# The last store of a batched q·kᵀ kernel, issued as a DMA of three quarters of every row and two for the rest, of 125 and 3 partitions

## The chip, the cores and the metric

One core of a Trainium2 chip. The metric is the device time of one execution, in microseconds (us); lower is better.

## The reference

```python
q, k: (8, 12, 1024, 64) float32
def reference(q, k):
    return np.einsum('bhid,bhjd->bhij', q, k).astype(np.float32)
```

That is 96 heads, each a 1024 x 1024 product over 64. The output is 402.65 MB, the input 50.33 MB: a kernel that mostly writes.

## The kernel before

Inputs are loaded and cast to float16, transposed on VectorE, multiplied on TensorE, copied from PSUM by ScalarE into an output tile of 32 KB per partition, and each finished head goes out as one 4 MB store on the SyncE queue. Three output tiles rotate. What matters here:

```python
out_pool = ctx.enter_context(tc.tile_pool(name="out_pool", bufs=3))
...
def scores(self, n, side):
    ...
    o_sb = out_pool.tile([P, NT, S], F32, tag="out")     # 128 x 8 x 1024
    for u in range(NT // 2):
        ...                                              # 4 matmuls into ps
        pin(nc.scalar.copy(out=dst, in_=ps))             # all but the first heads
        ...
    pin(
        nc.sync.dma_start(
            out=of[self.first + n].rearrange("(p t) j -> p (t j)", p=P),
            in_=o_sb.rearrange("p t j -> p (t j)"),
        )
    )
```

Row 8p + t of a head lies in partition p, so each partition's row of 8192 elements is contiguous in memory on both sides.

## Time and profile before

| | before |
|---|---|
| time | 1066.99 us, median of 3 runs (1066.63 to 1067.32) |
| span of the profiled core | 1065.3 us |
| DMA | 425 GB/s mean over the span, 430 GB/s in the steady part |
| busiest compute engines | PE 66%, ScalarE 65% |
| last store issued, first and last of its 16 landings, end of span | 1042.44, 1053.39, 1063.95, 1065.30 us |

A DMA of this kernel is spread over up to 16 DMA engines. In the traces an engine's packets follow one another, and after the last comes a 4-byte completion write, whose landing raises the semaphore of the DMA by one. The trace keeps the time of every such landing, so the landings of one DMA show when each of its engines finished, but not which engine it was. In the views, a DMA share of 1.00 means all 16 engines are busy, 0.06 is one engine.

### The profile page before, as it was taken

How to read it: one execution, taken by the hardware profiler on the slowest of the kernel's cores; microseconds unless marked ns; L12 is line 12 of the kernel's file. 1: busy time of each engine (PE TensorE's matmuls, PEld its weight loads, DVE VectorE, ACT ScalarE, POOL GpSimd, SP SyncE). 2: the span in 40 equal slices, each digit the busy share in tenths (PEclk: the TensorE clock that was granted, in tenths of full speed). 3: DMA queues.
4: the chain of work that ended last, by engine and by line, in shares of the span. 5: the costliest groups of instructions: out<-in, count | busy, mean ns of one | idle time of the engine just before them, and what ended most of it. 6: DMA issues, size and time to landing. Idle time of an engine off the chain costs nothing.

```text
span 1065.3 us, 4306 instructions
## 1 busy us (share of the span) xinstructions
PE 700.8 (66%) x1568; PEld 240.8 (23%) x1568; DVE 427.0 (40%) x57; ACT 694.5 (65%) x384; POOL 354.5 (33%) x206
## 2 busy tenths in 40 slices
PE   5886757667576665766667566675766757778770
PEld 2222222222222222222222222222222222222220
DVE  3767750480191084058029108405702910940000
ACT  2776667576675766757666675666757667777771
POOL 7666350523505225052250532505325053200000
DMA  9999999999999999999999999999999999999996
GB/s 381 433 430 432 429 433 432 432 429 432 431 426 435 430 428 431 431 430 430 431 429 431 432 429 428 432 431 429 430 431 429 430 429 433 431 432 428 431 433 273
DMA packets 27382, 453.28 MB, mean 425 GB/s; under 512 B 3040, under 2 KB 3040, under 8 KB 14304
## 3 DMA queue, kind: packets, MB, share of 16 engines
q1 hardware_dynamic: 15120, 407.90, 89.0%
q10 hardware_dynamic: 12240, 45.09, 10.4%
q8 instruction: 12, 0.20, 0.1%
q14 instruction: 10, 0.08, 0.0%
HBM read 50.33 MB, written 402.65 MB: 425 GB/s over the span
## 4 chain that ended last, share of the span: by engine, by line
DMA 71%; ACT 17%; PE 7%; POOL 1%; DVE 1%; issue 1%; ACTq 0%; POOLq 0%
DMA out_dram<-o_sb 70%; ACT o_sb L169 17%; PE ps L158 7%; POOL half_sb L114 1%; DMA early<-in_k_dram 1%; DVE kT L131 0%; DVE o_sb L165 0%; DVE o_sb L167 0%; ACT o_sb L164 0%; ACT L164 0%; ACTq L169 0%; DVE kT L142 0%; PE ps L139 0%; ACTq L77 0%; POOLq L114 0%
## 5 line engine op out<-in xcount | busy, mean ns | idle before, releaser
L158 PE MATMUL ps<-kT,qT 64*128 64x512 f16 x1536 | 696.9, 617 | 333.1 <-ACT o_sb L169 326.2
L169 ACT COPY o_sb<-ps 128x2048 f32<-128x2048 f32 x379 | 689.2, 1869 | 333.3 <-DMA out_dram<-o_sb 303.9
L114 POOL CAST half_sb<-x_sb 32x2048 f16<-32x2048 f32 x176 | 332.5, 1889 | 549.9 <-DMA x_sb<-in_k_dram 517.5
L158 PEld LDWEIGHTS <-qT 64*128 64x128 f16 x1536 | 237.4, 157 | 790.7 <-issue 788.4
L131 DVE STREAM_TRANSPOSE qT<-half_sb 128x2048 f16<-128x2048 f16 (+1 forms) x24 | 213.2, 8884 | 496.6 <-POOL half_sb L114 496.6
L131 DVE STREAM_TRANSPOSE kT<-half_sb 128x2048 f16<-128x2048 f16 (+1 forms) x24 | 215.7, 8988 | 0.0
L114 POOL CAST half_sb<-early 32x1024 f16<-32x1024 f32 x16 | 16.6, 1036 | 2.2 <-DMA early<-in_k_dram 1.5
L164 ACT ACT_TABLE_LOAD x1 | 1.3, 1283 | 11.7 <-DMA early<-in_k_dram 11.7
L139 PE MATMUL ps<-ident,half_sb 128*128 128x128 f16 x32 | 3.9, 309 | 6.6 <-POOL half_sb L96 6.1
L165 DVE COPY o_sb<-ps 128x1024 f32<-128x1024 f32 x4 | 4.8, 1222 | 6.9 <-ACT o_sb L164 6.9
L96 POOL CAST half_sb<-early 128x512 f16<-128x512 f32 x8 | 4.7, 616 | 3.8 <-DMA early<-in_q_dram 3.8
L164 ACT COPY o_sb<-ps 128x1024 f32<-128x1024 f32 x4 | 4.0, 1014 | 3.0 <-PE ps L158 3.0
L142 DVE COPY qT<-ps 128x1024 f16<-128x1024 f16 x2 | 2.4, 1220 | 7.1 <-PE ps L139 7.1
L139 PEld LDWEIGHTS <-half_sb 128*128 128x128 f16 x32 | 3.3, 142 | 8.1 <-POOL half_sb L96 6.1
L142 DVE COPY kT<-ps 128x1024 f16<-128x1024 f16 x2 | 2.4, 1220 | 3.8 <-PE ps L139 3.8
L167 DVE COPY o_sb<-ps 128x2048 f32<-128x2048 f32 x1 | 2.3, 2291 | 2.0 <-PE ps L158 2.0
masks.py:199 POOL TENSOR_SCALAR_AFFINE_SELECT ident<-ident 128x128 f16<-128x128 f16 x1 | 0.3, 294 | 0.1
masks.py:197 POOL MEMSET ident<- 128x128 f16 x1 | 0.2, 205 | 0.3 <-POOLq L277 0.3
L277 POOL MEMSET const-float32-0.0<- 128x1 f32 x1 | 0.1, 98 | 0.2 <-issue 0.2
L277 POOL MEMSET const-bfloat16-1.0<- 128x1 bf16 x1 | 0.1, 102 | 0.0
L277 POOL MEMSET const-uint8-127<- 128x1 uint8 x1 | 0.1, 102 | 0.0
L277 POOL MEMSET const-float32-1.0<- 128x1 f32 x1 | 0.1, 98 | 0.0
## 6 DMA issues: line engine op xcount, KB each, us to landing
out_dram<-o_sb SPq DMA_DIRECT2D x96, 4096.0 KB, 25.6
x_sb<-in_q_dram ACTq DMA_DIRECT2D x38, 512.0 KB, 24.7
x_sb<-in_k_dram ACTq DMA_DIRECT2D x38, 512.0 KB, 24.7
x_sb<-in_q_dram SPq DMA_DIRECT2D x3, 1024.0 KB, 14.7
x_sb<-in_k_dram ACTq DMA_DIRECT2D x3, 1024.0 KB, 15.2
early<-in_q_dram SPq DMA_DIRECT2D x4, 256.0 KB, 4.9
early<-in_k_dram ACTq DMA_DIRECT2D x4, 256.0 KB, 5.0
early<-in_q_dram SPq DMA_DIRECT2D x2, 512.0 KB, 7.6
```

Source lines behind the costliest of these rows:

```text
L96: nc.gpsimd.tensor_copy(out=self.halves[x][:, :, half], in_=self.raw[half][:, x].rearrange("p (r d) -> p r d", d=D),)
L114: nc.gpsimd.tensor_copy(out=dst[:, :, b % 2], in_=raw[32 * b : 32 * b + 32, :, :, h],)
L131: pin(nc.vector.transpose(out=dst, in_=src))
L139: pin(nc.tensor.transpose(t_ps[:, t], self.halves[x][:, t], ident))
L142: pin(nc.vector.tensor_copy(out=dst, in_=src))
L158: nc.tensor.matmul(ps[:, tt, js], qT[cs, g, 2 * u + tt], kT[cs, g, js])
L164: pin(nc.scalar.copy(out=dst[:, 0], in_=ps[:, 0]))
L165: pin(nc.vector.tensor_copy(out=dst[:, 1], in_=ps[:, 1]))
L167: pin(nc.vector.tensor_copy(out=dst, in_=ps))
L169: pin(nc.scalar.copy(out=dst, in_=ps))
L277: nc = _bacc.Bacc("TRN2", target_bir_lowering=False, num_devices=1)
```

## The change

Its intent can be read from its shape: at the end of the program the engines stop one after another, and a quarter of the last store is taken from all 16 and given to a few.

```diff
-            pin(
-                nc.sync.dma_start(
-                    out=of[self.first + n].rearrange("(p t) j -> p (t j)", p=P),
-                    in_=o_sb.rearrange("p t j -> p (t j)"),
-                )
-            )
+            dst = of[self.first + n].rearrange("(p t) j -> p t j", p=P)
+            parts = [(slice(P), slice(NT))]
+            if self.first + n == BH - 1:
+                rest = slice(NT - 2, NT)
+                parts = [
+                    (slice(P), slice(NT - 2)),
+                    (slice(125), rest),
+                    (slice(125, P), rest),
+                ]
+            for ps, ts in parts:
+                pin(nc.sync.dma_start(out=dst[ps, ts], in_=o_sb[ps, ts]))
```

The other 95 stores, and every instruction of the compute engines, stay as they are.

## The prediction

> **What bounds the kernel now.** I read the page first, part 2 (the span in 40 slices), then the DMA queues and issues, then the chain of waits, and last the end of the span in narrow windows.
>
> ```profile
> DMA  9999999999999999999999999999999999999996
> GB/s 381 433 430 432 429 433 432 432 429 432 431 426 435 430 428 431 431 430 430 431 429 431 432 429 428 432 431 429 430 431 429 430 429 433 431 432 428 431 433 273
> DMA packets 27382, 453.28 MB, mean 425 GB/s; under 512 B 3040, under 2 KB 3040, under 8 KB 14304
> ...
> DMA 71%; ACT 17%; PE 7%; POOL 1%; DVE 1%; issue 1%; ACTq 0%; POOLq 0%
> ...
> out_dram<-o_sb SPq DMA_DIRECT2D x96, 4096.0 KB, 25.6
> ```
>
> The 16 DMA engines are over 90% busy in 39 of 40 slices at about 430 GB/s, while no compute engine is above 66%. The bytes are fixed: 402.65 MB of output and 50.33 MB of input. So the only time that is not already filled with transfers is at the two ends, and the fortieth slice (6 tenths, 273 GB/s) is the end the change works on. Cut into windows of the trace (columns: stretch in us, its length, busy time and count of PE, PEld, DVE, ACT, POOL, clock, DMA share, GB/s), that slice looks so:
>
> ```profile
> 1052.00:1053.00 1.00, 0.00 (x0) 0.00 (x0) 0.00 (x0) 0.00 (x0) 0.00 (x0) 1.00 0.91 393
> 1053.00:1054.00 1.00, 0.00 (x0) 0.00 (x0) 0.00 (x0) 0.00 (x0) 0.00 (x0) 1.00 0.69 295
> 1054.00:1056.00 2.00, 0.00 (x0) 0.00 (x0) 0.00 (x0) 0.00 (x0) 0.00 (x0) 1.00 0.49 213
> 1056.00:1058.00 2.00, 0.00 (x0) 0.00 (x0) 0.00 (x0) 0.00 (x0) 0.00 (x0) 1.00 0.27 115
> 1058.00:1060.00 2.00, 0.00 (x0) 0.00 (x0) 0.00 (x0) 0.00 (x0) 0.00 (x0) 1.00 0.15 66
> 1060.00:1062.00 2.00, 0.00 (x0) 0.00 (x0) 0.00 (x0) 0.00 (x0) 0.00 (x0) 1.00 0.04 16
> 1062.00:1064.00 2.00, 0.00 (x0) 0.00 (x0) 0.00 (x0) 0.00 (x0) 0.00 (x0) 1.00 0.04 16
> ```
>
> Nothing computes any more, and the DMA share falls in steps for ten microseconds. It is not one transfer slowing down; it is 16 engines stopping one after another. The trace's record of semaphore landings says the same more sharply. The last store lands 16 times, once per engine, at 1053.39, 1053.42, 1053.46, 1053.86, 1053.95, 1054.96, 1055.19, 1055.26, 1055.83, 1056.12, 1057.38, 1058.06, 1058.44, 1059.93, 1060.54 and 1063.95 us. The store before it shows nearly the same spread, 1043.64 to 1054.30, so the order of the engines is a lag built up over the whole kernel, and each engine takes about 9.7 us for its 256 KiB. One engine is 3.41 us behind the second slowest, and alone it sets the end. The last instruction of the queue and the wait that ends the program:
>
> ```profile
> 1042.44 0.33 SPq L173 DMA_DIRECT2D out_dram<-o_sb  x1
> ...
> SPq L288 <- DMA out_dram<-o_sb: 21.1, 3, 9.6
> ```
>
> The store is issued at 1042.44, before even the fastest engine has finished the one before it (1043.64), so no engine runs dry. After the last landing 1.35 us remain to the end of the span at 1065.30 (closing barrier).
>
> **What the Trainium skill says.** First, "DMA: Bandwidth & Descriptors", section "Why a DMA increments its semaphore by 16 and not by 1": a DMA uses the largest k up to 16 that divides the slowest dimension of both sides, on the lowest-numbered k engines; 127 partitions give 1. The trace agrees for 128 partitions: 96+38+38+3+3+4+4+2+2 = 190 DMAs times 16 completion writes are the 3040 packets under 512 B. By that rule 125 partitions go to 5 engines (0 to 4) and 3 to 3 engines (0 to 2); no DMA of the kernel before tests it. Second, the same page, "Latency and other measured facts": engines 7 and 15 are usually slower than the others, with a cause that the page calls a guess and ties to another kind of queue. The trace shows one clear laggard but not its number. Third, "SBUF — State Buffer", "Door 1: The DMA port swizzle": eight partitions share one DMA port of about 27.2 GB/s, and a 128-partition transfer gives each engine a port of its own. The packet records agree with the rate: 32,768 B in 1.213 us (median) is 27.0 GB/s. They can't say whether the engine or the port sets it, and that matters below.
>
> **The change part by part.** The order of instructions shows 95 stores untouched, and the ninety-sixth replaced by three DMAs on the same queue: 128x6144, 125x2048 and 3x2048 elements. PE, ACT, DVE and POOL keep their instructions. Everything up to 1042.4 us should be as before.
>
> Removed: each engine's eight 32 KB packets become eight of 24 KB. At 1.213 us per 32 KB that is 0.909 us each, 8 x 0.304 = 2.43 us less on each of the 16 engines.
>
> Added, on engines 0 to 4: 25 packets of 8 KB. The trace has 384 packets of 8 KB on this queue (loads), median 0.313 us, so 7.83 us. Engines 0 to 2 get one more, 0.31 us. Net per engine: 5 to 15 -2.43 us; 3 and 4 +5.40; 0 to 2 +5.71.
>
> Added, on the issuing side: two more issues of 0.33 us at 1042.8 and 1043.1. Their data is needed only when an engine has done its 24 KB packets, over 7 us later: hidden. Their two semaphores were last used eight DMAs earlier, so no wait. The closing waits name these semaphores already; I allow 0.1 us.
>
> Sum, if engines 0 to 4 are the five early ones (there are exactly five within 0.56 us, then a gap of 1.0): laggard 1063.95 - 2.43 = 1061.52; second slowest 1058.11; the five at most 1053.95 + 5.71 = 1059.66. The laggard still ends last, with 1.9 us to spare. The end moves by -2.43 us plus 0.1: 1064.66 us, -0.22%. The most that perfect balance could give is the laggard's distance to the mean of the 16 landings (1056.46), 7.5 us or 0.7%. So a gain over 2% (21 us) is impossible through this part of the time.
>
> **The rivals.**
> *The wrong engines.* Nothing in this profile numbers the engines. An engine that gets +5.71 stays under 1061.52 only if it landed before 1055.81, which eight of sixteen do. If one of the five is today's 1057.38, the end is 1063.1 (gain 0.9); at 1058.44 it is 1064.2 (+0.2); at 1060.54 it is 1066.3 (+2.3, time 1069.3); if the laggard itself is one, +5.7 and a time of 1072.7. For it: five drawn blindly would mostly include a late one. Against it: a split as odd as 125 and 3 looks chosen to reach the five engines known to be early, and the skill's usual slow ones are 7 and 15.
>
> *The ports.* The five engines now read partitions outside their own port. If the rate is the port's and not the engine's, bytes per port are unchanged: the laggard's port has 256 KiB left at 1054.30 as before, whoever reads them, and while the laggard is busy every visitor slows it. Then the gain vanishes: about 0, time 1067.0, and if the five are held up by busy ports, up to 1 to 3 us slower. For it: 27.0 measured is within 1% of the page's port figure. Against it: an engine may have the same limit, and both then look alike; no transfer of the kernel before crosses ports.
>
> *One engine only.* If the rule gave k = 1 for 125 partitions, 125 x 0.313 = 39.1 us would sit on one engine: 1053.4 - 2.4 + 39.1 = 1090.1 for an early one, +26 us, a time near 1093, slower by 2.4%. 125 = 5 x 25, so the rule speaks against it; I leave 2%.
>
> *Hidden anyway?* No: nothing but this store runs after 1042.4, so what the laggard gains is gained.
>
> **Range and chances.** I give the full gain (about 1064.6) 45%; a part of it, through one misplaced engine or partial port sharing (1065 to 1066.8), 15%; no gain by ports (about 1067) 20%; a loss of 1 to 6 us 18%; one engine only 2%. The median lies just above the full gain: 1065.2. Eight in ten: 1064.0 to 1069.5; the low end is the full gain with 0.6 us for spread between runs (0.7 us in the three runs before), the high end takes in all but the worst placements. Faster by over 2% is excluded by the 7.5 us bound; 0.5% stays for what I don't see. Slower by over 2% needs the one-engine case: 2%.
>
> **What would show it.** In the changed kernel's profile: packets 27382 - 144 + 280 = 27518 (280 = 128 + 125 + 3 data and 16 + 5 + 3 completion writes), and 3048 under 512 B instead of 3040, if k is 5 and 3; 3042 would mean k = 1 twice. The 6144-element store should take 16 landings ending near 1061.5, some 2.4 us sooner, and the 125-partition one five landings between 1058.8 and 1059.7. Placement wrong: the five landings come after 1061.5 and set the end. Ports: the five land late and spread out, the 16 gain less than 2.4 us, and 8 KB packets on the queue take clearly more than 0.313 us, up to twice that. The windows after 1060 should have more than one engine's share (0.06) if the load is better spread.

## The result, and the profile after

The changed kernel takes 1073.09 us (median of 4 runs, 1072.15 to 1073.29), against 1067.0 us (4 runs) of the kernel before. The ratio is 1.0055, 95% interval 1.0038 to 1.0073, so it is slower by half a per cent. Here and below a ratio is the mean time of one kernel's fast runs over the mean of the other's of the same rounds, so it is not quite the ratio of the medians. The forecast of 1065.2 us and its range of 1064.0 to 1069.5 both missed.

The page of the changed kernel, parts 2 (the slices), 4 (the chain that ended last, by engine) and 6 (the DMA issues):

```profile
DMA  9999999999999999999999999999999999999994
GB/s 381 441 427 431 430 429 436 425 432 430 432 435 425 434 426 435 433 428 432 429 430 427 429 439 422 434 433 425 433 427 433 427 434 434 430 432 432 429 429 188
DMA packets 27518, 453.28 MB, mean 423 GB/s; under 512 B 3048, under 2 KB 3048, under 8 KB 14312
...
DMA 71%; ACT 17%; PE 7%; POOL 1%; DVE 1%; issue 1%; ACTq 0%; POOLq 0%
...
out_dram<-o_sb SPq DMA_DIRECT2D x95, 4096.0 KB, 25.5
...
out_dram<-o_sb SPq DMA_DIRECT2D x1, 3072.0 KB, 21.5
```

Slices 2 to 39 are as full as before. The chain has the same shares. Only the fortieth slice differs, 188 GB/s in place of 273, so the 5 us of the span are lost at the very end. The packet counts are those that the prediction worked out for 5 and 3 engines (27518 and 3048), so the 125-partition piece did go to five engines.

The same stretch in windows (columns as in the prediction; the two last are DMA share and GB/s):

```profile
1052.00:1053.00 1.00, 0.00 (x0) 0.00 (x0) 0.00 (x0) 0.00 (x0) 0.00 (x0) 1.00 0.56 197
1053.00:1054.00 1.00, 0.00 (x0) 0.00 (x0) 0.00 (x0) 0.00 (x0) 0.00 (x0) 1.00 0.50 172
1054.00:1056.00 2.00, 0.00 (x0) 0.00 (x0) 0.00 (x0) 0.00 (x0) 0.00 (x0) 1.00 0.54 193
1056.00:1058.00 2.00, 0.00 (x0) 0.00 (x0) 0.00 (x0) 0.00 (x0) 0.00 (x0) 1.00 0.52 164
1058.00:1060.00 2.00, 0.00 (x0) 0.00 (x0) 0.00 (x0) 0.00 (x0) 0.00 (x0) 1.00 0.31 107
1060.00:1062.00 2.00, 0.00 (x0) 0.00 (x0) 0.00 (x0) 0.00 (x0) 0.00 (x0) 1.00 0.18 78
1062.00:1064.00 2.00, 0.00 (x0) 0.00 (x0) 0.00 (x0) 0.00 (x0) 0.00 (x0) 1.00 0.13 53
1064.00:1066.00 2.00, 0.00 (x0) 0.00 (x0) 0.00 (x0) 0.00 (x0) 0.00 (x0) 1.00 0.09 37
1066.00:1068.00 2.00, 0.00 (x0) 0.00 (x0) 0.00 (x0) 0.00 (x0) 0.00 (x0) 1.00 0.06 25
1068.00:1070.00 2.00, 0.00 (x0) 0.00 (x0) 0.00 (x0) 0.00 (x0) 0.00 (x0) 1.00 0.03 12
```

The tail is not shorter and better filled; it is longer, and it again ends with one engine alone: 0.06 from 1066 to 1068. The landing records say when each piece finished, and split the 5 us (us from the start of the span; store 96 is the last, store 95 the one before it):

```
kernel before    store 95: 1043.64 ... 1050.90 1054.30
                 store 96: 1053.39 1053.42 1053.46 1053.86 1053.95 1054.95 1055.19 1055.26
                           1055.83 1056.12 1057.38 1058.07 1058.44 1059.93 1060.54 1063.95
changed kernel   store 95: 1043.35 ... 1051.98 1054.59
   128 x 6144:   1050.72 1050.73 1050.82 1050.84 1050.94 1051.30 1051.32 1051.35
                 1051.40 1052.63 1052.88 1056.15 1059.24 1059.81 1060.06 1061.84
   125 x 2048:   1060.36 1060.48 1062.06 1064.92 1069.43
     3 x 2048:   1060.79          1062.36 1065.24
```

Three of the five engines show the third piece about 0.3 us after their share of the second. The engine that ends at 1069.43 has no third piece, so it is engine 3 or 4 if pieces sit on the lowest-numbered engines. And 1069.43 minus 25 packets at just over 0.3 us is 1061.8, the landing of the slowest engine's first piece, 1061.84. So already this trace suggests that the laggard is one of the five.

The changed kernel's last issues, from its timeline (start, us, engine, line, operation, count):

```profile
1040.38 3.26 SPq L184 DMA_DIRECT2D out_dram<-o_sb  x3
```

And the SyncE queue's longest wait from 1035 us on (us in total, times, longest):

```profile
SPq L295 <- DMA out_dram<-o_sb: 25.7, 4, 10.2
```

All three pieces are issued by 1043.6, long before any engine can start the second piece (the first landing of the first piece is 1050.72). The first piece went out at 1040.38, 2 us before the store of the kernel before (1042.44): the issue came before the last copies into the tile had ended. The prediction had it at 1042.4; as no engine had finished store 95 by then, it gained nothing. The closing waits on the stores grew from 21.1 to 25.7 us in total. Issuing costs nothing; waiting for the last landing does.

### The profile page after: what moved, and what is told of

It reads as the page before. It is cut to its first block, busy times and chain, and to the rows that moved or that the text cites. A ratio compares the mean times of both kernels' runs of the same rounds, so it can differ in the third digit from the quotient of the medians.

```text
span 1070.3 us, 4309 instructions
## 1 busy us (share of the span) xinstructions
PE 701.2 (66%) x1568; PEld 240.7 (22%) x1568; DVE 427.1 (40%) x57; ACT 695.0 (65%) x384; POOL 354.4 (33%) x206
## 2 busy tenths in 40 slices
DMA packets 27518, 453.28 MB, mean 423 GB/s; under 512 B 3048, under 2 KB 3048, under 8 KB 14312
## 4 chain that ended last, share of the span: by engine, by line
DMA 71%; ACT 17%; PE 7%; POOL 1%; DVE 1%; issue 1%; ACTq 0%; POOLq 0%
DMA out_dram<-o_sb 70%; ACT o_sb L169 17%; PE ps L158 7%; POOL half_sb L114 1%; DMA early<-in_k_dram 1%; DVE kT L131 0%; DVE o_sb L165 0%; DVE o_sb L167 0%; ACT o_sb L164 0%; ACT L164 0%; ACTq L169 0%; DVE kT L142 0%; PE ps L139 0%; ACTq L77 0%; POOLq L114 0%
```

## The experiments

Theory 1, after the result: the laggard, the engine that lands last and so sets the end of the kernel before, is one of the five engines that got more. Two rivals: the loss comes from reading partitions outside an engine's own port, whoever does it (theory 2); or it comes from splitting the store at all (the third theory).

### Naming the engines: mark_1_to_5, mark_6_to_10, mark_11_to_15, mark_again

Tiny loads into a tile that nobody reads are queued behind the last store of the kernel before. A load on k engines lands once per engine, right after that engine's share of the store. Each load adds one engine to those of the one before, so the new landing names a new engine. The traces show that the sets nest; the numbers 0, 1, 2 and so on come from the rule that the prediction quotes, lowest-numbered engines first, since no trace numbers an engine.

```diff
             to_half(i + 2 + (n == heads - 1))
+    marks = consts.tile([P, 5, P], F32)
+    for i, rows in enumerate([17, 2, 3, 4, 5]):      # 6..10 and 11..15 in the others
+        pin(nc.sync.dma_start(
+            out=marks[:rows, i],
+            in_=qf[: 2 * rows].rearrange("(p r) d -> p (r d)", r=2)))
```

> The kernel before, with five tiny loads queued behind the last store, of 17, 2, 3, 4 and 5 partitions of 512 B into a scratch tile that nobody reads. If a DMA of k engines sits on the lowest-numbered k (17 partitions: one engine), their landings name engines 0 to 4, since each load starts on an engine only when that engine has done its share of the last store. Theory 1 (the laggard is among the five): the changed kernel's last landing of the 125-partition store, 1069.43, minus 25 packets of 0.303 us is 1061.85, which is the laggard's own landing of the 24 KB part (1061.84); and the three engines with a third piece are the ones that end at 1060.8, 1062.4 and 1065.2. So the laggard is engine 3 or 4: the load on 3 engines ends early, at most 1060.6, and the load on 4 or on 5 is the first whose last landing comes with the laggard's, near 1064. Theory 2 (the five are early, the ports made the loss): all five loads land by about 1056, and the laggard is in none of them. Time within 0.3 us of the kernel before, both theories.

> The same with loads on 6, 7, 8, 9 and 10 engines, to name engines 5 to 9. Theory 1: every one of these loads contains the laggard (engine 3 or 4) and so lands last near 1064, each with one more landing than the one before it. Theory 2: at least the load on 6 engines lands before the laggard; it appears from some k on or not at all. Time within 0.3 us of the kernel before.

> The same with loads on 11 to 15 engines, to name engines 10 to 15 (engine 15 is the one in none of them). Theory 1: all five land last with the laggard, near 1064, and engine 15 is not it. Theory 2, in the form that the skill suggests (engine 15 or 7 slow): the load on 15 engines lands last by 1060.6, without the laggard, if it is 15. Time within 0.3 us of the kernel before.

All three gave right results, at 1067.56, 1068.63 and 1068.36 us (one run each; the kernel before beside them 1067.18, median of 7), 0.4, 1.5 and 1.2 us above the kernel before instead of within the 0.3 expected. In the last two each of the five loads contains the laggard and lands after it, the last one 0.95 us after the store; that accounts for most of it (1064.82 and 1065.77; 1064.55 and 1065.49). The landings of the first:

```
store 96 (16 engines): 1053.39 1053.40 1053.41 1053.44 1053.51 1053.76 1053.90 1053.92
                       1053.95 1054.02 1054.69 1055.00 1056.41 1057.54 1057.60 1064.51
17 partitions: 1054.14
 2 partitions: 1054.33 1054.87
 3 partitions: 1053.59 1054.51 1055.04
 4 partitions: 1053.62 1053.77 1054.68 1055.21
 5 partitions: 1053.80 1053.94 1054.86 1055.39 1064.70
```

17 partitions give one landing, so they ran on one engine. Each further load repeats the earlier landings (0.2 us later, behind the earlier loads) and adds one. The engine added by the fifth load, engine 4, is the laggard: 1064.70, when the others of the five had finished by 1055.4. The loads on 6 to 10 and 11 to 15 engines all land last with the laggard too (1065.01 to 1065.77 and 1064.74 to 1065.49). They also place engines 7 and 15: the load on 8 engines adds a landing at 1053.94, among the early ones; and of the seven engines that had finished the store by 1054.48 in the third run, the load on 15 engines shows only six, so engine 15, which it leaves out, is an early one.

> The marked kernel before once more (engines 0 to 4). Engine 4 again lands last, at 1064 to 1065. If engines 0 to 3 keep their place (the order is a fixed property of each engine), they land within 0.5 us of the first marked run, 1053.4 to 1055.0; if it changes between executions, at least one of them moves by over 1 us, which would explain why the runs on engines 0 to 3 scatter and the kernel before, whose end is engine 4's, does not.

The repeat took 1067.14 us and answers whether the order is fixed:

```
                engine 0  engine 1  engine 2  engine 3  engine 4
mark_1_to_5     1054.14   1054.87   1053.59   1053.62   1064.70
mark_again      1055.00   1057.85   1056.05   1054.91   1064.28
```

(Each is the engine's landing in the first load that contains it.) Engine 4 is last in both. Engines 0 to 3 move: engine 1 by 3.0 us, engine 2 by 2.5. But the record lists chip 1 for the first run and chip 7 for the repeat (and for after_marked and quarter_k4_marked below), so this pair alone can't tell a change between executions from one between chips. The trace of one_tile_k4 below, on chip 1 too, can: there two of engines 0 to 3 landed store 95, before anything was split, only at 1050.04 or later, where in mark_1_to_5 no engine but the laggard landed it after 1047.93. So engines 0 to 3 are not equally early in each execution, and engine 4 was the last of the five on both chips.

### The split alone: split_16

```diff
-                    (slice(125), rest),
-                    (slice(125, P), rest),
+                    (slice(0, 128), rest),
```

> The split alone: three quarters of every row and the remaining quarter, both of 128 partitions, so that all 16 engines share the quarter as they did. Theory 1 (placement on five engines is the cost): as the kernel before, 1067.0 plus at most 0.5 us, since 128 packets of 32 KB become 128 of 24 KB and 128 of 8 KB at the same rate. A third theory (splitting a store, smaller packets, the extra DMA and its wait cost the 6 us): most of the 6 us stays, 1071 to 1073. Theory 2 (ports) also says 1067, since each engine stays on its own port.

1067.28 us against 1067.18 of the kernel before, ratio 1.0001 (0.9985 to 1.0018). Splitting, smaller packets and one DMA more are free here; that rival is out. Its profile is also the comparison for the ports. In windows of split_16:

```profile
1054.00:1056.00 2.00, 0.00 (x0) 0.00 (x0) 0.00 (x0) 0.00 (x0) 0.00 (x0) 1.00 0.70 299
1056.00:1058.00 2.00, 0.00 (x0) 0.00 (x0) 0.00 (x0) 0.00 (x0) 0.00 (x0) 1.00 0.44 184
```

In the second line 0.44 of the engines move 184 GB/s, which is 418 GB/s per full share (184 / 0.44). The changed kernel in the same window moves 164 GB/s at 0.52, only 315 (164 / 0.52): its engines are busy but slowed. The packets agree. In split_16 no 8 KB packet of the last store takes over 0.324 us and no 24 KB packet over 1.194; in the changed kernel 8 KB packets take up to 1.418 us (median 0.309) and 24 KB packets up to 1.882, just over double the usual 0.912. So packets on both sides, the 24 KB and the 8 KB ones, are slowed when a few engines read partitions that are not theirs. That they meet at a partition's port is the likely reading; a meeting on the memory side was not tested. What remains is whether this sets the end.

### One partition moved: quarter_k4

```diff
-                    (slice(125), rest),
-                    (slice(125, P), rest),
+                    (slice(0, 124), rest),
+                    (slice(124, 128), rest),
```

> The changed kernel with its quarter cut at partition 124 in place of 125: 124 = 4 x 31 rows on engines 0 to 3, and the other 4 rows one each on the same four. The markers put the laggard at engine 4. Theory 1 (the loss is that the laggard is one of the five): one partition moved takes nearly the whole 6 us away. The laggard loses 2.43 us and ends near 1061.5 to 1062.4; engines 0 to 3, which landed the last store by 1055.2 in the marked run, get 31 x 0.309 + 0.309 - 2.43 = +7.5 us and end at 1061 to 1063, or up to 2 us later where they wait for ports (three of the five did so by 1.2 to 1.6 us in the changed kernel). Time 1065 to 1068. Theory 2 (reading other partitions' ports is the loss, whoever does it): four engines that each read more rows across ports are no better than five, 1073 or above.

Four timed runs gave 1067.35, 1067.62, 1071.68 and 1072.03 us (median 1069.65; the kernel before 1067.05, median of 11; ratio 1.0024, 1.0009 to 1.0040). Two runs are where theory 1 puts them, two are not. The profiled one is 1067.62:

```profile
1058.00:1060.00 2.00, 0.00 (x0) 0.00 (x0) 0.00 (x0) 0.00 (x0) 0.00 (x0) 1.00 0.30 94
1060.00:1062.00 2.00, 0.00 (x0) 0.00 (x0) 0.00 (x0) 0.00 (x0) 0.00 (x0) 1.00 0.26 102
1062.00:1064.00 2.00, 0.00 (x0) 0.00 (x0) 0.00 (x0) 0.00 (x0) 0.00 (x0) 1.00 0.11 41
1064.00:1066.00 2.00, 0.00 (x0) 0.00 (x0) 0.00 (x0) 0.00 (x0) 0.00 (x0) 1.00 0.02 8
```

Several engines now work together until 1062 (0.26 is four), and no piece lands after 1064.95: the three quarters end at 1062.21, the four at 1061.30, 1062.73, 1063.21 and 1064.65. Moving the cut by one partition took away, in this execution, most of the stretch in which one engine worked alone: the last two shares of the quarter land 1.4 us apart, against 4.5 us in the changed kernel (1064.92 and 1069.43). The two slow runs have no trace, so I ran the kernel marked.

> The run with 124 and 4 partitions, marked in the same way: which engine ends last there. It gave two values, 1067.4 to 1067.6 and 1071.7 to 1072.0. If the place of engines 0 to 3 changes from one execution to the next while engine 4 stays, the four landings of the 124-partition store differ by several us from those of the profiled run before (1061.3 to 1064.7), engine 4's own part lands near 1062 all the same, and the time is either about 1067.5 or up to 1072.

That run took 1070.54 us, and the loads name its last engine: the load on 1 engine lands at 1063.72, the load on 2 adds 1067.21, which is engine 1 (its share of the 124 rows 1066.72). Engine 4 is seen at 1062.38, well before. So without the laggard in the group the end was set by one of engines 0 to 3 that happened to be late; the kernel is then at the mercy of an order that changes from run to run. I take the two slow runs (on chip 1) for the same case, but only this run (on chip 7) shows it. Theory 2 in its plain form, as bad as 125 or worse every time, is refuted by the two runs at 1067.

### Half the dose, with and without engine 4: one_tile_k5, one_tile_k4

```diff
-                rest = slice(NT - 2, NT)
+                rest = slice(NT - 1, NT)
...
-                    (slice(P), slice(NT - 2)),
-                    (slice(125), rest),
-                    (slice(125, P), rest),
+                    (slice(P), slice(NT - 1)),
+                    (slice(0, 125), rest),      # one_tile_k4: 124
+                    (slice(125, 128), rest),    # one_tile_k4: 124
```

> Half the dose: one eighth of every row (one tile, 4 KB) goes as 125 and 3 partitions, seven eighths as 128. Theory 1: the laggard, engine 4, loses 1.21 us and gets 25 packets of 4 KB at 0.156 to 0.159 us, 3.95 us, so +2.7 us, less the 0.4 us by which the closing waits were shorter in the changed kernel: 1069.3 to 1070. If instead the loss came from having an extra DMA on few engines, whatever its size, it stays near 1073.

1070.66 us (1069.76 to 1071.13), ratio 1.0033 (1.0020 to 1.0046): between the kernel before and the changed one, as theory 1 says, but 0.7 us above the top of what I expected. Its profiled run, 1071.13 us, shows where the excess is. Engine 4 gained only 0.60 us on its 28 KB packets rather than 1.21: an 8 KB instruction fetch sat between them (0.309 us) and the packet behind it took 1.328 us instead of 1.062. And its 25 packets of 4 KB took 5.10 us and not 3.95, because seven of them took 0.186 to 0.606 us instead of 0.159. So slow packets did reach the laggard here, for about 1.2 us. Six of the seven (0.9 us) ran while other engines were still at work. The seventh, 0.567 us from 1065.51 on, did not: no other packet is in flight in the trace then. So meeting other engines explains at most a part, and what slowed that one is open.

> One eighth of every row as 124 and 4 partitions, on engines 0 to 3, without the laggard. Theory 1: the laggard loses 1.21 us and gets nothing back; engines 0 to 3 get 31 x 0.158 + 0.158 - 1.21 = +3.8 us and stay below 1060. Time 1065.8, about 1.2 us (0.1%) under the kernel before and 4 us under the run with 125 and 3 of the same size. Theory 2: 1068 or more, as the rows across ports are the same in number.

Five runs: 1065.95, 1066.33, 1066.43, 1068.87 and 1068.89 us. The first three are the gain that theory 1 gives, against 1067.05; the other two are not. The median is 1066.43, 4.2 us under one_tile_k5, which moves the same bytes with one more engine; against the kernel before the ratio is 1.0002 (0.9990 to 1.0014), so no gain is proven. The profiled run was one of the slow ones, and there the 124 rows land at 1059.03, 1059.04, 1065.12 and 1066.06, the last two on engines that finished their 28 KB packets only at 1060.21 and 1060.43.

### A share between the two: three16_k4

The quarter becomes three sixteenths (6 KB of every row, cut inside a tile) with 124 and 4 partitions.

```diff
-                rest = slice(NT - 2, NT)
+                cut = NT * S - 3 * S // 2
+                rest = slice(cut, NT * S)
```

> Three sixteenths of every row (6 KB) as 124 and 4 partitions: the share at which the laggard and the four should end about together. Theory 1: laggard -1.82 us, engines 0 to 3 31 x 0.233 + 0.233 - 1.82 = +5.6 us, so at most 1061 without port waits. Time 1065.2, the best of the four, if port waits add less than 1.5 us to the four engines; otherwise 1065.8 to 1067. Theory 2: 1069 or more.

1069.97 us (1067.24 to 1072.48, six runs), ratio 1.0025 (1.0013 to 1.0037). My expectation of 1065.2 assumed that engines 0 to 3 are always as early as in the first marked run. In the profiled run, 1070.28 us, the laggard ends its 26 KB packets at 1062.72, but the four land at 1060.29, 1062.28, 1062.94 and 1067.42. As an improvement it failed, for the reason that mark_again and quarter_k4_marked show.

### The changed kernel, marked: after_marked

> The changed kernel with the five tiny loads (17, 2, 3, 4 and 5 partitions) queued behind its three pieces, to name the engines of the 125-partition store in the changed kernel itself. Theory 1 (engine 4, the laggard, ends last): the loads on 1 to 4 engines all land before the last landing of the 125-partition store, and only the load on 5 engines lands after it, near 1069 to 1071. If another engine had become the last one by port waits, a load on fewer engines lands there too. Time as the changed kernel, 1072 to 1074.

```
125 x 2048:      1059.08 1059.85 1061.16 1065.01 1069.77
  3 x 2048:              1060.15 1061.47 1065.31
load, 4 engines: 1059.26 1060.49 1062.39 1065.82
load, 5 engines: 1059.44 1060.66 1062.56 1065.99 1069.96
```

1072.81 us. Engines 0 to 3 are done at 1065.82; only the load on five engines adds a landing at 1069.96, behind 1069.77. Engine 4 alone sets the end of the changed kernel. The loads on one and two engines say that engine 1 is the second last (1065.48).

## Why the prediction was wrong

**What bounds the kernel, and what the tail is: right.** The body of the span stayed full, and only the last slice changed. One engine sets the end, before and after.

**Five engines and three: right.** 27518 packets and 3048 small ones, as worked out.

**Issue cost hidden: right.** All issued by 1043.6 (the first piece 2 us sooner than forecast, at 1040.38); splitting alone moved nothing (1.0001).

**"If engines 0 to 4 are the five early ones": this step failed.** The prediction noted that nothing in the profile numbers the engines, and then let the oddness of the split and a general remark on which engines are slow decide. In fact engine 4 is the laggard: mark_1_to_5, mark_again and after_marked all name it. The rival was worked out ("if the laggard itself is one, +5.7 and a time of 1072.7"), and the result of 1073.09 is 0.4 us from it. That closeness is partly luck: the prediction's own sum for engine 4 is +5.40 (5.71 holds for engines 0 to 2), the profiled run moved by 5.07, and the other three by up to 1.1 us more, which the prediction has no term for. The rival was given too little weight (18% for every loss of 1 to 6 us together), and the range stopped at 1069.5, "all but the worst placements". It was the worst placement that came.

**The sum for that case, term by term**, in the profiled runs of before and after. The laggard's landing of store 95 is 0.29 us later (1054.59 against 1054.30; an 8 KB instruction fetch lies in its stream in the changed kernel, 0.309 us, with a packet of 1.479 us in place of 1.213 behind it, and not in the kernel before). Its three quarters take 7.25 us where the whole took 9.65: -2.40 (predicted -2.43). Its 25 rows of 8 KB add 7.59 (predicted 7.83). Together +5.48: 1063.95 becomes 1069.43. From the last landing to the end of the span it takes 0.92 us rather than 1.35, -0.43, so closing costs less and not the 0.1 more that I allowed. The fetch and the shorter closing (0.92 us) are both in split_16 too, so neither comes from the placement. That makes +5.05, the difference of the spans (1070.35 and 1065.30). The times of these two runs differ by 5.07. The other three runs of the changed kernel are 0.9 to 1.1 us longer and have no trace; slowed packets of engine 4, as one_tile_k5 shows them, would do that, but nothing shows it for them.

**The port rival: a slowing is there, its place was wrong.** Where a few engines read partitions that are not theirs, 24 KB packets fall to about half their rate in the changed kernel, and split_16, whose pieces are both of 128 partitions, shows nothing of the kind; that ports are the reason stays inferred. But in the changed kernel's trace all 25 of the laggard's 8 KB packets took 0.309 us: it began them at 1061.38, when two other engines were still at work. The prediction had the ports take the gain from a laggard outside the group. Where the laggard was outside, with four engines, the 24 KB part of it ended 1.6 to 1.7 us sooner than in the kernel before (1062.21 and, with the load behind it, 1062.38, against 1063.95), so most of the 2.43 was in fact gained there, and then partly or wholly lost on engines 0 to 3.

**The bound on any gain: not contradicted.** The best run seen is 1065.95, 1.1 us under the kernel before, and not reliably. (The mean of the 16 landings that the prediction lists is 1056.48 and not 1056.46; the bound of 7.5 us stands.)

What stays open: why engine 4 lags. Its packets at the end of the kernel before take the usual 1.213 us, and its share of the bytes is that of the others. The spread of a store's landings grows over the kernel, from 2.2 us at 147 us to 6.0 at 478 and 10.6 at the end. Instruction fetches explain little of it: the laggard's lag behind the middle of the 16 landings grows by about 0.1 us per store, with one step of 0.7 us (3.13 to 3.85) at the store in whose time a fetch at 379.31 us falls. No run here tells the cause of the rest. The runs lie on two chips, 1 and 7 (the record doesn't say which one the first result came from); engine 4 was last on both, and no run shows more chips.

## What to carry to other kernels

When one of 16 DMA engines sets the end, find out which one before shifting work: a few tiny DMAs on growing numbers of engines behind the last transfer name them in one run. A DMA of 125, 124, 17 or 3 partitions went to 5, 4, 1 and 3 engines here, always to the same first ones, whether they were early or late, so work taken from all and given to k engines makes the laggard worse if it is among them, here by 7.6 us for 2.4 gained. And a tail whose end is one steady laggard hides the scatter of the other engines; once it is relieved, the scatter shows up in the time.

## What the Trainium skill lacked or had wrong

- "DMA: Bandwidth & Descriptors", "Latency and other measured facts", calls engines 7 and 15 usually slower, in a note that it ties to another kind of queue. For these stores it pointed the wrong way: in both marked runs of the kernel before that name engine 4, it was last (1064.70 and 1064.28). In one other run each, engine 7 was done by 1053.94 (mark_6_to_10) and engine 15 by 1054.48 (mark_11_to_15).
- The same page, "Why a DMA increments its semaphore by 16 and not by 1", has the rule for k right: 125, 124, 17 and 3 partitions ran on 5, 4, 1 and 3 engines. It doesn't say what follows for a tail: engines that carry equal bytes ended up to 10.6 us apart (1053.39 to 1063.95), so the lowest-numbered ones are not a safe place for extra work.
- "SBUF — State Buffer", "Door 1: The DMA port swizzle", gives the rate of a port, and the page says elsewhere that DMA engines can contend at these ports when they write; it has no figure for engines of two DMAs that meet there, and nothing on reads. In the changed kernel, where five engines read partitions that are not theirs, packets of 24 KB took up to 1.882 us instead of 0.912, and 8 KB packets up to 1.418 instead of 0.309. That the port is the meeting point is inferred: the trace doesn't number ports.
- No page has the cost of an instruction fetch to the DMA engine that it lands on ("Runtime: NRT & Kernel Launch", "Instruction fetch mechanics", describes fetches from the side of the sequencer alone): 0.309 us for 8 KB, and 0.27 us more on the packet behind it (1.479 against 1.213 us).
